# Layer 0's two products as seven block products, one level of Strassen's identity

## The chip, the cores and the metric

The kernel runs on one core of one Trainium2 chip. The metric is the device time of one execution in microseconds; a run of the program gives one such time, and the figure of the kernel is the median of its runs.

## The reference, cut to what matters

Two layers over 1,088 tokens of width 1,024: 1,024 tokens of a prompt and 64 of a running stream. Layer 0 is a gated short convolution, layer 1 an attention over latents, which the change leaves as it is.

```
h = rms_norm(x, norm_g[0])
b_gate, c_gate, xv, z = split(h @ w_in, 4)         # w_in: 1024 x 4096
u = c_gate * xv
conv = up[0:T]*cw[0] + up[1:T+1]*cw[1] + up[2:T+2]*cw[2]   # up: two earlier rows, then u
y = (silu(z) * b_gate * conv) @ w_out              # w_out: 1024 x 1024
x1 = x + y
```

All of it is in float32, and the result has to be as exact as that. TensorE's fast float32 form (fp32r) keeps fewer bits, so the kernel splits each operand into a high part (a cast to fp32r) and a low part (the operand less the high part) and makes every product of three: high by high, high by low, low by high.

## The kernel before, in words

Features lie on the 128 partitions and tokens along the free axis. `XH` and `XL` hold the high and low part of x times the norm's gain, eight tiles of 128 features by 1,088 tokens, resident in SBUF. The tokens are worked on in three chunks of `CHK`: 384, 384 and 320.

Layer 0's input product runs over eight column tiles `ct` and in each over the four parts of w_in in the order 1, 2, 3, 0 (c_gate, xv, z, b_gate). `load_w` brings a weight tile of 128x1024 by DMA (512 KB), ScalarE casts it to the high part (L288) and GpSimd subtracts to give the low part (L292). For each chunk a chain of 24 matmuls (8 feature tiles by 3 products, all through `mm`, L298) sums into one PSUM bank. `conv_evac` (L432 to L467) takes the bank: VectorE multiplies by the norm's factor or by the part before (L440, L451, L457), ScalarE applies silu, two VectorE steps make the convolution (L464), L465 multiplies it by the gate, and the gated result is split into `YH` (ScalarE, L466) and `YL` (GpSimd, L467), which stay in SBUF.

The output product has eight tiles `dt` of one weight tile and three chains of 24 each (`gemm`). Behind each chain VectorE adds the residual from PSUM (L551), and the sum is split into layer 1's `XH` (ScalarE, L552) and `XL` (VectorE, L553, two tensors from SBUF); squares for layer 1's norm are summed at L559.

Nothing is written out by hand here but the start (the first column tile, under `keep_order`): elsewhere the framework's scheduler orders each engine's instructions, and waits follow from data and from buffers (`wraw` has three, `whi` and `wlo` two).

## Time and profile before

| | |
|---|---|
| time, median of 3 runs | 1116.67 us (1116.12 to 1116.78) |
| profiled execution, span | 1115.8 us |
| TensorE (PE), busy | 1075.0 us, 96% |
| VectorE (DVE), busy | 626.8 us, 56% |
| ScalarE (ACT), busy | 502.7 us, 45% |
| GpSimd (POOL), busy | 407.5 us, 37% |
| DMA | 93.18 MB, mean 84 GB/s |

The profiled execution's own time is its span, from its first instruction to its last. PE is the queue of matmuls, PEld that of weight loads beside it. A row that groups instructions names the line, the engine, the operation, the tile written and those read, the shapes, the count, then busy time and the mean of one in ns, and at last the idle time ahead of them with what ended it.

### The profile page before, as it was taken

What the parts mean: (1) busy time and instruction counts of PE and PEld (TensorE: products, weight loads), DVE (VectorE), ACT (ScalarE), POOL (GpSimd) and SP (SyncE); (2) the same over time, 40 slices, a digit from 0 to 9 for tenths busy, and PEclk for the clock granted to TensorE, in tenths of its full rate; (3) what the DMA queues carried; (4) which work ended last, traced back from release to release, by engine and by line L of the source; (5) the groups of instructions that cost most, each with busy time, mean ns of one, the idle gap of its engine ahead of it and who ended that gap; (6) DMA issues with size and microseconds to landing.
All of it is one profiled execution on the core that took longest, in us unless ns stands there. A gap on an engine that the chain in (4) does not pass through costs nothing.

```text
span 1115.8 us, 17727 instructions
## 1 busy us (share of the span) xinstructions
PE 1075.0 (96%) x6659; PEld 1033.5 (93%) x6659; DVE 626.8 (56%) x1277; ACT 502.7 (45%) x1077; POOL 407.5 (37%) x375
## 2 busy tenths in 40 slices
PE   8989999999999999999898999999999999999994
PEld 7989999999999999999798999899999999989983
DVE  6752222222322235554898442688888888896456
ACT  6512121221112133344442334777887778785452
POOL 3123232323324232122433232354555445463243
PEclk9989999999999999999998999999999999999997
DMA  6211111111112123322323113444323422434324
GB/s 228 67 38 39 57 38 43 53 38 50 46 38 77 40 78 139 137 94 90 105 101 124 48 35 86 119 91 103 68 59 91 95 61 51 104 123 151 99 83 153
DMA packets 45461, 93.18 MB, mean 84 GB/s; under 512 B 6672, under 2 KB 23824, under 8 KB 45376
## 3 DMA queue, kind: packets, MB, share of 16 engines
q1 hardware_dynamic: 45168, 91.73, 27.4%
q8 instruction: 52, 0.85, 0.3%
q14 instruction: 33, 0.27, 0.1%
q10 hardware_dynamic: 144, 0.26, 0.1%
q0 software_dynamic: 64, 0.07, 0.0%
HBM read 60.26 MB, written 14.08 MB: 67 GB/s over the span
## 4 chain that ended last, share of the span: by engine, by line
PE 75%; DVE 8%; issue 5%; ACT 4%; DMA 4%; POOL 2%; SPq 1%; POOLq 0%; DVEq 0%; ACTq 0%
PE PS L298 55%; PE PS L1088 16%; PE PS L1127 4%; DMA QB<-stg 2%; POOL wlo L1366 1%; DVE rb L401 1%; ACT PH L1140 1%; DVE PL L1144 1%; SPq L1214 1%; DVE OL L612 1%; DMA wraw<-in_w 1%; ACT stg L1204 1%; DVE qt L813 0%; DVE SZ L364 0%; DVE qt L818 0%
## 5 line engine op out<-in xcount | busy, mean ns | idle before, releaser
L298 PE MATMUL PS<-XH,whi 128*128 128x384 f32 (+1 forms) x984 | 324.2, 329 | 4.7 <-DVE SZ L632 3.9
L298 PE MATMUL PS<-XL,whi 128*128 128x384 f32 (+1 forms) x984 | 322.8, 328 | 0.8 <-DVE XL L392 0.8
L298 PE MATMUL PS<-XH,wlo 128*128 128x384 f32 (+1 forms) x984 | 321.3, 328 | 0.0
L292 POOL TENSOR_TENSOR wlo<-wraw,whi 128x1024 fp32r<-128x1024 f32 x56 | 135.9, 2427 | 301.0 <-ACT whi L288 297.9
L298 PEld LDWEIGHTS PS<-XH,whi 128*128 128x128 f32 x984 | 185.9, 189 | 6.1 <-issue 4.1
L298 PEld LDWEIGHTS PS<-XL,whi 128*128 128x128 f32 x984 | 185.9, 189 | 2.2 <-DVE XL L392 1.8
L298 PEld LDWEIGHTS PS<-XH,wlo 128*128 128x128 f32 x984 | 185.7, 189 | 0.2
L1088 PE MATMUL PS<-KB,QB 96*128 96x512 f32 (+11 forms) x576 | 125.1, 354 | 0.9 <-DVE SZ L632 0.6
L288 ACT CAST whi<-wraw 128x1024 fp32r<-128x1024 f32 (+1 forms) x57 | 59.3, 1040 | 140.4 <-PE PS L298 127.9
L1088 PEld LDWEIGHTS PS<-KB,QB 96*128 96x128 f32 (+1 forms) x576 | 94.4, 190 | 9.3 <-DVE PL L1144 1.1
L1105 DVE TENSOR_REDUCE st<-PS 128x1 f32<-128x1024 f32 (+7 forms) x128 | 94.6, 747 | 10.7 <-PE PS L1088 10.0
L1144 DVE TENSOR_TENSOR PL<-PS,PH 128x512 fp32r<-128x512 f32 (+3 forms) x192 | 98.8, 547 | 3.2 <-ACT PH L1140 1.8
L1122 POOL TENSOR_SCALAR Pt<-Pt,st 128x640 f32<-128x640 f32 (+3 forms) x64 | 61.4, 961 | 85.9 <-DVE st L1118 85.3
L1140 ACT CAST PH<-PS 128x512 fp32r<-128x512 f32 (+3 forms) x192 | 85.3, 496 | 14.6 <-PE PS L1127 13.2
L1088 PE MATMUL PS<-PH,VB 128*128 128x256 f32 x320 | 76.4, 278 | 0.1
L1088 PE MATMUL PS<-PL,VB 128*128 128x256 f32 x320 | 75.2, 281 | 0.2 <-DVE PL L1144 0.2
L1114 ACT ACTIVATE Pt<-PS,st 128x640 f32<-128x640 f32 (+3 forms) x64 | 62.0, 970 | 6.0 <-DVE st L1118 2.9
L298 PE MATMUL PS<-YL,whi 128*128 128x384 f32 (+1 forms) x192 | 63.0, 328 | 0.0
L298 PE MATMUL PS<-YH,whi 128*128 128x384 f32 (+1 forms) x192 | 63.0, 328 | 0.0
L298 PE MATMUL PS<-YH,wlo 128*128 128x384 f32 (+1 forms) x192 | 63.0, 328 | 0.0
L1088 PEld LDWEIGHTS PS<-PH,VB 128*128 128x128 f32 x320 | 60.7, 190 | 1.3 <-DVE PL L1144 0.8
L1088 PEld LDWEIGHTS PS<-PL,VB 128*128 128x128 f32 x320 | 61.0, 191 | 0.7 <-DVE PL L1144 0.4
(339 smaller groups left out, 1963.9 us busy)
## 6 DMA issues: line engine op xcount, KB each, us to landing
wraw<-in_w SPq DMA_DIRECT2D x64, 512.0 KB, 3.4
KB<-stg SPq DMA_DIRECT2D x32, 256.0 KB, 3.9
QB<-stg SPq DMA_DIRECT2D x32, 256.0 KB, 4.3
xr<-in_xT SPq DMA_DIRECT2D x8, 544.0 KB, 4.2
x_scratch<-xr SPq DMA_DIRECT2D x8, 544.0 KB, 2.7
QB<-qr_scratch SPq DMA_DIRECT2D x32, 128.0 KB, 2.9
x<-x_scratch SPq DMA_DIRECT2D x8, 416.0 KB, 3.2
xst<-in_xT SPq DMA_DIRECT2D x16, 192.0 KB, 3.7
```

Source lines behind the costliest of these rows:

```text
L288: ins = A.copy(out=hi[:, :n], in_=raw[:, :n])
L292: ordered((lo_engine or G).tensor_sub(lo[:, :m], raw[:, :m], r32(hi[:, :m])))
L298: ins = PE.matmul(ps, lhsT, rhs, start=start, stop=stop)
L401: ordered(V.tensor_add(rb[:, c0:c1], rb[:, c0:c1], q))
L612: ordered((lo_engine or V).tensor_sub(lo, src, r32(hi)))
L1088: pin(PE.matmul(ps, lhsT, rhs, start=start, stop=stop))
L1105: pin(V.tensor_reduce(out=st[:, 0:1], in_=TL["S", h, i], axis=AX.XY, op=ALU.max, negate=True))
L1114: pin(A.activation(out=Pt, in_=TL.pop(("S", h, i)), func=AF.Exp, bias=st[:, 0:1], accum_out=st[:, 1:2]))
L1122: pin(G.tensor_scalar(Pt, Pt, st[:, 2:3], 1.0, op0=ALU.mult, op1=ALU.mult))
L1127: pin(PE.transpose(out=tp[:, j * P:(j + 1) * P], in_=TL["P", h, i][:, (j0 + j) * P:(j0 + j + 1) * P], identity=ident))
L1140: pin(A.copy(out=hi, in_=src))
L1144: pin(V.tensor_sub(lo, src, r32(hi)))
```

## The change

The tokens are cut into two halves `SC` of 544, each half into two quarters `NS` of 272, the features into two halves of four tiles, and the columns into pairs of weight tiles. On such a two by two block matrix seven products stand in for eight (Strassen's identity in Winograd's form). The first two column tiles of the first token half are still made directly, now in chunks of 272. All else is 36 `Pair`s: 28 of the input product (parts 1 with 2, `put_u`; parts 3 with 0, `put_z`) and 8 of the output product (`out_pair`).

- `build` makes the seven sums of token blocks for each of four feature tiles, with high part (ScalarE) and low part (VectorE); for the input product from x with the norm already applied, for the output product from the DRAM scratch `y_scratch`, where `conv_tail` now writes the gated result.
- `prep` makes the sums of weights for a pair: two loads, three tiles t1, t2, t4 of 512 columns by four VectorE subtractions (L610, L611, L612, L617), and high and low parts of the two whole tiles and of the three sums. The low part of t2 is VectorE's, the four others are GpSimd's (all at L575).
- `product` issues 12 matmuls of 272 columns into one of four banks; p1, p6 and p7 share a bank that goes on summing and are copied to SBUF in between (L638, ScalarE). `put_u` and `put_z` add such a copy to a bank and multiply blocks.
- `run` sets the order: in pair n's turn p1, the last product p3 of pair n-1, p5, p6, p2, p7, p4, with the steps of the next pair's `prep` in between, and `side()` for the builds.
- Layer 1's operands are split behind the output product for the second token half and read back from DRAM for the first (`h_first`).

In layer 0, PE has 2,880 matmuls before (1,920 of 384 columns, 960 of 320), and 3,408 of 272 columns after.

```
+    NS = T // 4
+    SC = 2 * NS
+    REG = 14 * 4 * NS
...
+    y_d = nc.dram_tensor("y_scratch", (KD, P, T), F32, kind="Internal").ap()
...
-    YH = p1.tile([P, KD, T], F32R, name="YH")
-    YL = p1.tile([P, KD, T], F32R, name="YL")
-    rb = p1.tile([P, T], F32, name="rb")
-    rb2 = p1.tile([P, T], F32, name="rb2")
+    R2 = p1.tile([P, REG], F32R, name="R2")
+    SETS = [[R[:, i * REG // 2:(i + 1) * REG // 2].rearrange("p (s k n) -> p s k n", s=7, k=4) for i in range(2)]
+            for R in (R1, R2)]
...
+    def conv_tail(ct, sc, u, z, a, b):
+        n = b - a
+        cv = p1.tile([P, SC], F32, tag="cv", name=nm("cv"), bufs=1)[:, :n]
+        cw = [sm[:, C_CW + j * 8 + ct:C_CW + j * 8 + ct + 1] for j in range(3)]
+        ordered(A.activation(out=cv, in_=u[:, a:b], func=AF.Copy, scale=cw[0]))
+        for j in (1, 2):
+            ordered(V.scalar_tensor_tensor(cv, u[:, a + j:b + j], cw[j], cv, op0=ALU.mult, op1=ALU.add))
...
+        ordered(V.tensor_mul(cv, cv, z[:, a:b]))
+        SP.dma_start(out=y_d[ct][:, sc * SC + a:sc * SC + b], in_=cv)
...
+    def build(sc, k, src, norm):
+        h, l = [x[:, :, k] for x in SETS[sc]]
+        a, b = [STG[:, (2 * (k % 2) + i) * SC:(2 * (k % 2) + i + 1) * SC] for i in range(2)]
+        halves = lambda x: x.rearrange("p (s n) -> p s n", s=2)
+        def put(s, x):
+            o, ol = h[:, s:s + 2], l[:, s:s + 2]
+            A.copy(out=o, in_=halves(x))
+            V.tensor_sub(ol, halves(x), r32(o))
+        SP.dma_start(out=a, in_=src[k][:, sc * SC:(sc + 1) * SC])
+        SP.dma_start(out=b, in_=src[k + 4][:, sc * SC:(sc + 1) * SC])
+        if norm:
+            for x, kk in ((a, k), (b, k + 4)):
+                V.scalar_tensor_tensor(x, x, sm[:, C_NG + kk:C_NG + kk + 1], rb[:, sc * SC:(sc + 1) * SC], op0=ALU.mult, op1=ALU.mult)
+        yield
+        A.copy(out=h[:, 0], in_=a[:, :NS])
+        V.tensor_sub(l[:, 0], a[:, :NS], r32(h[:, 0]))
+        put(1, b)
+        yield
+        V.tensor_add(b[:, NS:], a[:, NS:], b[:, NS:])
+        V.tensor_sub(a[:, NS:], a[:, :NS], a[:, NS:])
+        V.tensor_sub(a[:, :NS], b[:, NS:], a[:, :NS])
+        V.tensor_sub(b[:, :NS], b[:, :NS], a[:, :NS])
+        yield
+        put(3, a)
+        put(5, b)
+        yield
...
+    def parts_of(hi, lo, src, eng):
+        A.copy(out=hi, in_=src)
+        eng.tensor_sub(lo, src, r32(hi))
+        return hi, lo
+    def unit(src):
+        units[0] += 1
+        pool, tags, bufs = (p1, ("bhi", "blo"), 1) if units[0] % 3 == 0 else (wp[0], ("whi", "wlo"), 2)
+        return parts_of(*(pool.tile([P, 1024], F32R, tag=x, name=nm(x), bufs=bufs) for x in tags), src, G)
...
+    def prep(f):
+        ra, rb_ = raw(), raw()
+        SP.dma_start(out=ra, in_=f.srcs[0])
...
+        def own(i):
+            return [p1.tile([P, 512], F32R, tag=f"t{i}{x}", name=nm(f"t{i}{x}"), bufs=1) for x in "hl"]
...
+        def give(u, *names):
+            for j, n in enumerate(names):
+                w[n] = [x[:, j * 512:(j + 1) * 512] for x in u]
+        yield
+        give(unit(ra), "p1", "p2")
+        yield
+        b12, b22 = rb_[:, :512], rb_[:, 512:]
+        b11, b21 = ra[:, :512], ra[:, 512:]
+        t1 = p1.tile([P, 512], F32, tag="t1", name=nm("t1"), bufs=1)
+        V.tensor_sub(t1, b12, b11)
+        V.tensor_sub(b12, b22, b12)
+        V.tensor_sub(b11, b22, t1)
+        give(parts_of(*own(1), t1, G), "p5")
+        yield
+        give(unit(rb_), "p7", "p3")
+        yield
+        V.tensor_sub(b21, b21, b11)
+        give(parts_of(*own(2), b11, V), "p6")
+        give(parts_of(*own(4), b21, G), "p4")
+        yield
...
+    BANK = dict(p1=0, p6=0, p7=0, p2=1, p5=2, p3=2, p4=3)
+    def product(f, name):
+        i = BANK[name]
+        wh, wl = f.w[name]
+        for sc, b in f.banks:
+            ps = PS[:, 4 * b + i, :NS]
+            sh, sl = [x[:, POS[name]] for x in SETS[sc]]
+            for k in range(4):
+                ws = slice(k * P, (k + 1) * P)
+                new = name in ("p1", "p2", "p4", "p5")
+                mm(ps, wh[:, ws], sh[:, k], k == 0 and new, False, not new)
+                mm(ps, wh[:, ws], sl[:, k], False, False, not new)
+                mm(ps, wl[:, ws], sh[:, k], False, k == 3, not new)
+            if i == 0:
+                t = f.tmp[sc, name] = p1.tile([P, NS], F32, tag="k" + name, name=nm(name), bufs=1)
+                A.copy(out=t, in_=ps)
+                if f.early:
+                    f.early(sc, name, t)
+            if name == "p2":
+                f.put(sc, 11, f.tmp[sc, "p1"], ps)
+            elif name == "p7":
+                f.put(sc, 22, t, PS[:, 4 * b + 2, :NS])
+            elif name == "p4":
...
+                f.put(sc, 12, f.tmp[sc, "p6"], ps)
...
+        for n, f in enumerate(pairs):
+            if f.begin:
+                f.begin()
+            while f.whole and jobs:
+                side()
+            product(f, "p1")
+            side()
+            if n:
+                product(pairs[n - 1], "p3")
+                pairs[n - 1].end()
+            step(n + 1)
+            product(f, "p5")
+            side()
+            product(f, "p6")
+            side()
+            step(n + 1)
+            product(f, "p2")
+            side()
+            step(n + 1)
+            product(f, "p7")
+            side()
+            product(f, "p4")
+            side()
+            step(n + 1)
+            step(n + 2)
...
+        def put_u(sc, block, x, ps):
+            q = quarter(block)
+            o = st["u", sc][:, q.start + 2:q.stop + 2]
+            if block % 10 == 1:
+                V.tensor_add(o, x, ps)
+                if ("t", sc, q.start) in st:
+                    V.tensor_mul(o, o, st.pop(("t", sc, q.start)))
+                else:
+                    st["d", sc, q.start] = True
+            else:
+                t = p1.tile([P, NS], F32, tag="t", name=nm("t"), bufs=2)
+                V.tensor_add(t, x, ps)
+                if ("d", sc, q.start) in st:
+                    V.tensor_mul(o, o, t)
+                else:
+                    st["t", sc, q.start] = t
...
+        def end_u():
+            for sc in scs:
+                conv_state(ct, sc, st["u", sc])
+        def end_z():
+            for sc in scs:
+                conv_tail(ct, sc, st["u", sc], st["z", sc], 0, SC)
+            if ct == KD - 1:
+                jobs.extend(build(scs[0], k, y_d, False) for k in range(4))
...
-    for ct in range(KD):
...
+    for ct in range(2):
...
+    jobs.append(second_half())
+    single = lambda cts, sc: [f for ct in cts for f in conv_pairs(ct, [sc])]
+    pairs = single(range(2, KD), 0) + single(range(KD), 1)
...
+    def h_first():
+        for dt in range(KD):
+            x = p1.tile([P, SC], F32, tag="cv", name=nm("hx"), bufs=1)
+            SP.dma_start(out=x, in_=x1_d[dt][:, :SC])
+            h_split(dt, 0, SC, x)
+            yield
...
+        def early(sc, name, t):
+            if name == "p1":
+                G.tensor_add(xr[0][:, :NS], xr[0][:, :NS], t)
+        def put(sc, block, t, ps):
+            a, j = block // 10 - 1, block % 10 - 1
+            dt = 2 * q + j
+            x = xr[j][:, a * NS:(a + 1) * NS]
+            if block != 11:
+                V.tensor_add(x, x, t)
+            V.tensor_add(x, ps, x)
+            c0 = sc * SC + a * NS
+            SP.dma_start(out=x1_d[dt][:, c0:c0 + NS], in_=x)
+            if sc == 1:
+                h_split(dt, c0, c0 + NS, x)
+            if c0 not in begun:
+                begun.add(c0)
+                A.activation(out=acc1[:, c0:c0 + NS], in_=x, func=AF.Square)
+            else:
+                s = p1.tile([P, NS], F32, tag="t", name=nm("sq"), bufs=2)
+                A.activation(out=s, in_=x, func=AF.Square)
+                V.tensor_add(acc1[:, c0:c0 + NS], acc1[:, c0:c0 + NS], s)
...
+    pairs += [out_pair(q, sc) for sc in range(2) for q in range(4)]
+    for i in (12, len(pairs) - 8, len(pairs) - 4):
+        pairs[i].whole = True
+    run(pairs)
...
-    for dt in range(KD):
-        wh, wl = load_w(w2[dt], 1024)
-        xr = p1.tile([P, T + 4], F32, tag="u", name=nm("xr"), bufs=2)
-        SP.dma_start(out=xr[:, :T], in_=xT[dt])
...
-        for c, (c0, c1) in enumerate(CHK):
-            n = c1 - c0
-            ps = gps()
-            gemm(ps[:, :n],
-                 lambda k: wh[:, k * P:(k + 1) * P], lambda k: wl[:, k * P:(k + 1) * P],
-                 lambda k: YH[:, k, c0:c1], lambda k: YL[:, k, c0:c1], KD)
-            V.tensor_add(xr[:, c0:c1], ps[:, :n], xr[:, c0:c1])
-            at = A.activation(out=XH[:, dt, c0:c1], in_=xr[:, c0:c1], func=AF.Copy, scale=g)
-            V.scalar_tensor_tensor(XL[:, dt, c0:c1], xr[:, c0:c1], g, r32(XH[:, dt, c0:c1]), op0=ALU.mult, op1=ALU.subtract)
```

GpSimd's order, before, around one weight tile of the input product (`wlo` is a weight tile's low part, `YL` the gated result's, one row for each chunk):

```order
L292 TENSOR_TENSOR wlo_168_2531<-wraw_166_2529,whi_167_2530 128x1024
L453 TENSOR_TENSOR z_158_2417<-z_158_2417,rb_105 128x320
L467 TENSOR_TENSOR YL_104<-cv_162_2451,YH_103 128x384
L467 TENSOR_TENSOR YL_104<-cv_163_2483,YH_103 128x384
L292 TENSOR_TENSOR wlo_171_2613<-wraw_169_2611,whi_170_2612 128x1024
```

And in the change, for one pair and the start of the next (`t1l` and `t4l` are low parts of weight sums, `blo` is a third buffer for a weight tile's low part):

```order
L575 TENSOR_TENSOR wlo_235_2086<-braw_222_1993,whi_234_2085 128x1024
L575 TENSOR_TENSOR t4l_241_2125<-wraw_221_1992,t4h_240_2124 128x512
L575 TENSOR_TENSOR blo_247_2163<-wraw_242_2128,bhi_246_2162 128x1024
L575 TENSOR_TENSOR t1l_251_2197<-t1_249_2192,t1h_250_2196 128x512
L575 TENSOR_TENSOR wlo_253_2215<-wraw_243_2129,whi_252_2214 128x1024
L575 TENSOR_TENSOR t4l_259_2255<-wraw_242_2128,t4h_258_2254 128x512
```

The gated result's low part is gone from GpSimd; a pair has two whole low parts and two of half a tile.

VectorE's order in the change, at the turn of a pair of parts 1 and 2 (`wraw` and `braw` are the raw weight tiles in which the sums are made in place; p1, p6 and p7 are the copies from PSUM):

```order
L739 TENSOR_TENSOR t_226_2025<-p6_209_1924,PS_64 128x272
L741 TENSOR_TENSOR z_185_1732<-z_185_1732,t_226_2025 128x272
L472 TENSOR_TENSOR cv_227_2028<-cv_227_2028,z_185_1732 128x544
L612 TENSOR_TENSOR wraw_221_1992<-braw_222_1993,t1_231_2064 128x512
L617 TENSOR_TENSOR wraw_221_1992<-wraw_221_1992 128x512
L610 TENSOR_TENSOR t1_249_2192<-wraw_243_2129,wraw_242_2128 128x512
L575 TENSOR_TENSOR t2l_239_2121<-wraw_221_1992,t2h_238_2120 128x512
L611 TENSOR_TENSOR wraw_243_2129<-wraw_243_2129 128x512
L714 TENSOR_TENSOR u_223_1996<-p1_225_2011,PS_64 128x272
L721 TENSOR_TENSOR t_237_2103<-p7_236_2101,PS_64 128x272
```

Five operations of 512 columns that take two inputs from SBUF have come into VectorE's turn, between those that empty the banks.

ScalarE's order in the change, at the same place (`bhi`, `whi`, `t1h`, `t2h`, `t4h` are high parts):

```order
L638 COPY p1_225_2011<-PS_64 128x272
L574 CAST whi_228_2034<-wraw_221_1992 128x1024
L574 CAST t1h_232_2068<-t1_231_2064 128x512
L574 CAST t2h_238_2120<-wraw_221_1992 128x512
L638 COPY p6_230_2062<-PS_64 128x272
L574 CAST whi_234_2085<-braw_222_1993 128x1024
L638 COPY p7_236_2101<-PS_64 128x272
L574 CAST t4h_240_2124<-wraw_221_1992 128x512
```

The cast of t2 stands right ahead of the copy of p6; t2 is written by L612 into the raw tile that GpSimd's `wlo` of the same tile reads.

## Rows read from the trace of the kernel before

**Rows 1.** The page's head.

```profile
span 1115.8 us, 17727 instructions
```

**Rows 2.** The chain that ended last, in order of time: start, length, engine, line, count.

```profile
64.81 434.73 PE PS L298 x2622
```

**Rows 3.** Windows of layer 0: the first line names the columns.

```profile
core 0: us, PE busy (x) PEld busy (x) DVE busy (x) ACT busy (x) POOL busy (x), PEclk, DMA share, GB/s
6.00:20.00 14.00, 12.38 (x65) 10.88 (x64) 9.67 (x13) 9.35 (x19) 6.97 (x5) 1.00 0.80 284
60.00:65.00 5.00, 0.62 (x4) 0.35 (x4) 4.44 (x10) 1.14 (x2) 3.29 (x2) 0.84 0.23 71
65.00:70.00 5.00, 5.00 (x21) 5.00 (x22) 2.11 (x8) 1.30 (x4) 0.33 (x1) 0.50 0.23 85
...
100.00:400.00 300.00, 300.00 (x1822) 300.00 (x1821) 75.72 (x179) 58.33 (x91) 98.33 (x65) 1.00 0.15 48
```

**Rows 4.** PE's timeline, first matmuls of chains: start, us, line, shape.

```profile
146.88 0.33 PE L298 MATMUL PS<-XH,whi 128*128 128x384 f32 x1
...
151.04 0.31 PE L298 MATMUL PS<-XH,whi 128*128 128x320 f32 x1
...
154.56 0.34 PE L298 MATMUL PS<-XH,whi 128*128 128x384 f32 x1
...
719.55 0.28 PE L1088 MATMUL PS<-PH,VB 128*128 128x256 f32 x1
...
720.97 0.22 PE L1088 MATMUL PS<-PH,VB 128*128 128x128 f32 x1
```

**Rows 5.** Groups by line and shape in layer 0, from 0 to 520 us.

```profile
L292 POOL TENSOR_TENSOR wlo<-wraw,whi 128x1024 fp32r<-128x1024 f32 x39 | 93.5, 2398 | 238.4 <-ACT whi L288 238.4
L284 POOL TENSOR_TENSOR wlo<-wraw,whi 128x512 fp32r<-128x512 f32 x2 | 2.6, 1298 | 3.6 <-ACT whi L283 3.6
L288 ACT CAST whi<-wraw 128x1024 fp32r<-128x1024 f32 x39 | 41.0, 1051 | 123.2 <-PE PS L298 112.2 <-issue 11.1
L283 ACT CAST whi<-wraw 128x512 fp32r<-128x512 f32 x2 | 1.1, 617 | 0.7 <-DMA wraw<-in_w 0.7
L343 ACT COPY rb<-PS 128x384 f32<-128x384 f32 x2 | 0.9, 458 | 0.0
L465 DVE TENSOR_TENSOR cv<-cv,z 128x384 f32<-128x384 f32 x16 | 8.9, 558 | 0.6
L553 DVE SCALAR_TENSOR_TENSOR XL<-xr,sm,XH 128x320 fp32r<-128x320 f32 x8 | 18.7, 2344 | 6.9 <-ACT XH L552 6.9
L392 DVE SCALAR_TENSOR_TENSOR XL<-xst,sm,XH 128x320 fp32r<-128x320 f32 x8 | 4.3, 547 | 1.5 <-ACT XH L391 1.5
```

**Rows 6.** Timelines of VectorE and GpSimd at three places where both have work.

```profile
488.63 2.41 POOL L292 TENSOR_TENSOR wlo<-wraw,whi 128x1024 fp32r<-128x1024 f32 x1 [9.57 <-ACT whi L288]
489.04 2.34 DVE L553 SCALAR_TENSOR_TENSOR XL<-xr,sm,XH 128x320 fp32r<-128x320 f32 x1 [0.95 <-ACT XH L552]
...
1080.10 5.10 POOL L1366 TENSOR_TENSOR wlo<-wraw,whi 128x1024 fp32r<-128x1024 f32 x2 [2.58 <-ACT whi L1364]
1087.84 2.70 POOL L1366 TENSOR_TENSOR wlo<-wraw,whi 128x1024 fp32r<-128x1024 f32 x1
1082.96 8.94 DVE L1338 TENSOR_TENSOR X<-X,acc 128x384 f32<-128x384 f32 x5
...
1097.95 3.22 DVE L1338 TENSOR_TENSOR X<-X,acc 128x448 f32<-128x448 f32 x6
1097.95 5.42 POOL L1366 TENSOR_TENSOR wlo<-wraw,whi 128x1024 fp32r<-128x1024 f32 x1 [7.41 <-ACT whi L1364]
```

**Rows 7.** The same two engines, VectorE with one input from PSUM.

```profile
843.63 0.59 POOL L1122 TENSOR_SCALAR Ph<-Ph,st 128x384 f32<-128x384 f32 x1 [0.25 <-DVE st L1118]
843.79 0.69 DVE L1208 TENSOR_TENSOR stg<-PS,stg 128x512 fp32r<-128x512 f32 x1 [0.26 <-ACT stg L1204]
```

**Rows 8.** PE's waits from 0 to 70 us: releaser, total, count, longest.

```profile
PE PS L298 <- DVE rsy L330: 5.9, 2, 4.4
```

More of the change, by code (lines that the diff above doesn't have):

```diff
@@ new lines, with side, load_half @@
+    jobs = []
+    def side(n=1):
+        while n and jobs:
+            if next(jobs[0], 0) == 0:
+                jobs.pop(0)
+            else:
+                n -= 1
+    def load_half():
+        for k in range(KD):
+            x = STG[:, (k % 4) * SC:(k % 4 + 1) * SC]
+            SP.dma_start(out=x, in_=xT[k][:, SC:])
+            if k == 0:
+                A.activation(out=rb[:, SC:], in_=x, func=AF.Square)
+            else:
+                A.activation(out=x, in_=x, func=AF.Square)
+                V.tensor_add(rb[:, SC:], rb[:, SC:], x)
+            if k % 2:
+                yield
@@ new lines, in run, with step @@
+    def run(pairs):
+        bset = 0
+        steps = {}
+        for n, f in enumerate(pairs):
+            if len(f.scs) == 1:
+                f.banks = [(f.scs[0], bset)]
+                bset = 1 - bset
+            else:
+                f.banks = [(f.scs[0], 0), (f.scs[1], 1)]
+        def step(n, k=1):
+            for _ in range(k):
+                if n < len(pairs):
+                    if n not in steps:
+                        steps[n] = prep(pairs[n])
+                    next(steps[n], None)
+        step(0, 5)
+        step(1, 1)
+        for n, f in enumerate(pairs):
+            if f.begin:
[22 more added lines that the diff above has]
+            step(n + 2)
+        product(pairs[-1], "p3")
+        pairs[-1].end()
+        while jobs:
+            side()
@@ L475 @@
+    PARTS = [1, 2, 3, 0]
+    for ct in range(2):
+        u, z = new_u(ct, 0), new_z()
         if ct == 0:
@@ L497 @@
             pe_order[0] = True
-            held = {c: [] for c in range(3)}
+            held = {c: [] for c in range(2)}
             held[0].append(conv_mm(0, W[1], 3))
@@ L502 @@
                     x_square(0, k)
-                W[part] = load_w(w1[ct][part], 1024, into=(YH[:, 6 + part // 3, :1024], YL[:, 6 + part // 3, :1024]))
-            for c in range(3):
+                W[part] = load_w(w1[ct][part], 1024, into=[p1.tile([P, 1024], F32R, tag=x, name=nm(x), bufs=1) for x in ("bhi", "blo")] if part else
+                                 [R1[:, REG - n:REG - n + 1024] for n in (2048, 1024)])
+            for c in range(2):
                 for pi, part in enumerate(PARTS):
@@ L517 @@
                         for q in range(3):
-                            conv_evac(ct, u, zt, PARTS[q], c, held[c][q])
+                            conv_evac(ct, u, z, PARTS[q], c, held[c][q])
                     if pi == 3:
-                        conv_evac(ct, u, zt, part, c, held[c][3])
-            pe_order[0] = False
+                        conv_evac(ct, u, z, part, c, held[c][3])
             keep_order[0] = False
+            jobs.extend(build(0, k, xT, True) for k in range(4))
         else:
@@ L525, with second_half @@
                 W = load_w(w1[ct][part], 1024)
-                for c in range(3):
-                    conv_evac(ct, u, zt, part, c, conv_mm(c, W))
-    SP.dma_start(out=o_conv, in_=nconv.rearrange("p a b -> p (a b)"))
-    acc1 = const.tile([P, T], F32, name="acc1")
+                for c in range(2):
+                    conv_evac(ct, u, z, part, c, conv_mm(c, W))
+                    side(2)
+        conv_state(ct, 0, u)
+    while jobs:
+        side()
+    split_psum(g=(7, 8))
+    def second_half():
+        yield from load_half()
+        yield
+        yield
+        end = rstd([rb[:, SC:]], rb[:, SC:], D, SC)
+        yield
+        yield
+        yield
+        end()
+        yield
+        for k in range(4):
+            yield from build(1, k, xT, True)
+    jobs.append(second_half())
+    single = lambda cts, sc: [f for ct in cts for f in conv_pairs(ct, [sc])]
+    pairs = single(range(2, KD), 0) + single(range(KD), 1)
     parts = {}
@@ L662 @@
     held = latent_mm(0, 0)
-    sums(2, p3t.tile([P, 512], F32, tag="qt1", name=nm("act"), bufs=2))
+    for c in (1, 2):
+        sums(c, p3t.tile([P, 512], F32, tag="qt1", name=nm("act"), bufs=2))
     latent_evac(0, 0, held)
```

241 lines of the change are left out of this document (156 added, 85 removed).

## The prediction

> **What bounds the kernel now.** I read the page's head first, then the chain that ended last, then windows of layer 0, then single timelines for prices. The profiled execution's span is 1115.8 us [rows 1], 0.9 us under the median of 1116.67; the sum below is a difference, made against this execution, and is added to the median. The chain shows TensorE alone from 64.81 us for 434.73 us, so layer 0 ends at 499.5 us [rows 2]. In the window from 100 to 400 us PE is busy for all 300 us at granted clock 1.00 (2.4 GHz), while VectorE is busy for 75.72 and GpSimd for 98.33 [rows 3]. Layer 0 is therefore PE's, and VectorE and GpSimd together need 174 of 300 us. The reader should keep that sum in mind, since it is the one that the change moves.
>
> **What the change takes from PE.** From the first matmul of one chain of 24 to that of the next, PE needs 151.04 - 146.88 = 4.16 us at 384 columns, 173.3 ns each, and 154.56 - 151.04 = 3.52 us at 320, 146.7 ns each; twelve matmuls of 256 columns take 720.97 - 719.55 = 1.42 us, 118.3 ns each [rows 4]. Between 320 and 256 columns, 272 come to 118.3 + 16/64 x 28.4 = 125.4 ns. Layer 0's matmuls before: 1,920 x 173.3 + 960 x 146.7 = 473.5 us. After: 3,408 x 125.4 = 427.4 us. The difference is 46 us in favour of the change, not an eighth, because smaller matmuls cost more for each column and the first two column tiles of a half stay direct. A pair takes PE 84 x 125.4 = 10.5 us; the same work, two weight tiles on half of the tokens, takes 48 x 173.3 + 24 x 146.7 = 11.84 us before.
>
> **What it adds to GpSimd.** Each weight tile is now used for 544 tokens at a time and so is split twice. A pair has two low parts of 1,024 columns at 2,398 ns and two of 512 at 1,298 ns [rows 5]: 7.4 us, for 36 pairs 266 us. The direct column tiles add 8 x 2.4 = 19 us, and eight early adds and four multiplications of 272 columns some 0.7 us each (1,298 x 272 / 512) = 8 us. Together 293 us. By itself that would hide under 427 us of PE.
>
> **What it adds to VectorE.** I count only operations whose two inputs both lie in SBUF, in columns: prep 36 x 5 x 512 = 92,000; the 16 builds 16 x 11 x 272 = 48,000 for low parts and sums, and 9,000 for the norm; multiplications of blocks 56 x 272 = 15,000; the tails of the convolution 14 x 3 x 544 = 23,000; the output product's adds, squares and splits 23,000; the second half's squares 4,000; the start and the direct tiles 11,000. Together 225,000. The 384-column one took 558 ns by itself, 1.45 ns for each column [rows 5]: 327 us. Additions that read a bank come on top, some 70 us, and by themselves these too would hide.
>
> **Why the two don't hide.** At 489.04 us a 320-column L553 starts 0.41 us after a GpSimd low part of 2.41 us; it takes 2.34 us and ends 0.34 us after that. The mean of its eight is 2,344 ns, where the same operation in the start (L392) takes 547 [rows 5, 6]. From 1082.96 us five VectorE operations of 384 columns take 8.94 us beside GpSimd's stream, one getting through for each GpSimd operation, whose pitch is then 2.70 us. And at 1097.95 us six VectorE operations of 448 columns run in 3.22 us, while the low part that began with them takes 5.42 us, 3.02 more than the usual 2.40 [rows 5, 6]. So one engine works while the other stands. With one input from PSUM it isn't so: at 843.79 us such an operation took 0.69 us across the end of a GpSimd one [rows 7]. The additions that read a bank are free of it. Before the change this costs nothing: 174 us of 300 leave room. After it the shared path is a queue of its own.
>
> **Its price.** Three rows bound what a VectorE column costs on that path. In a row behind each other: 3.02 us / (6 x 448) = 1.12 ns, 253 us. As whole operations: 1.45 ns, 327 us. Taking turns with GpSimd: (2.70 - 2.40) us / 384 = 0.78 ns, 176 us [rows 5, 6]. There are some 590 such operations to 167 of GpSimd, so most stand behind another of their own; I take 1.12.
>
> The Trainium skill ("SBUF — State Buffer", section "Who interferes with whom") says that a VectorE instruction with two SBUF inputs contends with a GpSimd instruction that reads SBUF, and that whoever issues first holds the shared pair for the whole instruction. The trace agrees on who blocks whom; by "the whole instruction" the sum would go by 327 us, where the six operations in a row cost 1.12 ns and not 1.45, and the measurement decides.
>
> **The sum.** Shared path: 253 + 293 = 546 us. To this come about 6 us at the start, before the window in which the loads run at 284 GB/s [rows 3], and time in which neither can run because both wait for a ScalarE cast. In GpSimd's order for a pair every low part waits for its cast, and t1, t2 and t4 wait for VectorE ahead of it. Casts take 1,051 ns for a tile and 617 for half a one [rows 5]. The trace of before doesn't show how much stands bare: at least nothing, at most all five, 2 x 1.05 + 3 x 0.62 = 4 us for each pair, 143 us. I take one half-tile cast, 0.62 x 36 = 22 us, because the next pair's tiles are asked for a turn ahead. Layer 0 then ends at 546 + 6 + 22 = 574 us, 74.5 us after before's 499.5, and all that follows moves with it: **1116.7 + 74.5, about 1191 us.** PE, with 454 us of its own (499.5 - 46), waits some 120 us of this: behind a VectorE operation that is held stand the additions that empty the banks (L714, L721, L739 in VectorE's order), and PE's next product into that bank waits for them, as its products with t1, t2 and t4 wait for late low parts.
>
> Edits that cost nothing: the gated result's way through DRAM, since pairs lie between its writing and its reading and GpSimd gave up that low part; the loads, 1 MB for each pair in about 14 us, some 75 GB/s where 284 were moved in the window from 6 to 20 us [rows 3]; ScalarE, whose casts and copies of a pair come to about 2 x 1.05 + 3 x 0.62 + 3 x 0.4 = 5 us of work. If that cover goes, the shared path still is the longer.
>
> **Rivals.**
> *A, the other side: PE sets the pace.* The shared path decides only while a pair's share of it is over PE's 10.5 us. The conv pair's own is 7.4 us of GpSimd and about 3,630 columns, 4.1 us at 1.12: 11.5 us, near that point. The builds and the output product carry the rest. If the low parts and the sums overlapped more than rows 6 show, PE would decide: 1116.7 - 46 = 1071 without waits. ScalarE's order adds a wait: the cast of t2 stands ahead of the copy of p6 in 16 of the 36 turns, and before it come a 1.05 us cast, a 2.40 us low part, a VectorE subtraction of 512 x 1.45 = 0.74, the cast itself and the copy, 0.62 + 0.45 [rows 5], 5.26 us in all. If the chain begins behind p1 and p3 (24 x 0.125 = 3.0 us), it ends at 8.3 us of the turn, where p7 is due after 60 matmuls, at 7.5. That is 0.8 x 16 = 13 us. The first build in front of pair 0, some 4 x 4.6 us of VectorE, may cost another 8. So 1071 to 1092. Against it stands every row of 6. **Chance 0.11.**
> *B, the two engines mesh well.* Half of the columns go at the alternating price, 88 + 126 = 214 us, and no cast stands bare: 214 + 293 = 507, 7.5 us over before, 1124 us. The long run of turns at 1082.96 us speaks for it; that VectorE has three or four of its own in a row speaks against. **Chance 0.12.**
> *C, the clock falls too.* Behind a PE wait of 4.4 us [rows 8] the granted clock was 0.84 and in the next 5 us 0.50 (1.2 GHz) [rows 3], so half of 5 us was lost. In my forecast PE waits 120 / 36 = 3.3 us for each pair. If these waits come in one piece, the fall costs 2.5 us of PE in each turn, and since the copies, adds and buffers wait for PE in turn, half to all of it may come on top: 45 to 90 us, 1236 to 1281. Against it: in the window from 6 to 20 us, with 1.6 us of waits, the clock stayed at 1.00 [rows 3]. **Chance 0.12.**
> *D, whole operations and more bare casts.* With 1.45 ns for each column: 327 + 293 + 28 = 648, 148.5 over, 1265 us. **Chance 0.08.**
> *No change*, A's gain and the new waits cancelling: **0.04.** That the change wouldn't do what it says is ruled out by the count of matmuls.
>
> **How the numbers follow.** The forecast, 0.53, is 1191 us; its own bounds are B's 1124 and D's 1265. The range runs from 1124 to 1275: it leaves out A (0.11), no change (0.04) and the upper end of C (about 0.04). Over 0.2% (2.2 us, about what a measurement of this kernel can tell): faster 0.11, from A; same 0.04; slower 0.85, from the forecast, B, C and D.
>
> **What would show it.** Right: layer 0 ends near 574 us; PE is busy for some 75% of it, with waits for VectorE and ScalarE in every pair; the low parts of weights last well over 2.4 us, their mean 3 us or more; L610 to L617 show times of 2 us or more where GpSimd's run; L714 and L721, which read a bank, keep under 0.6 us when they start. Wrong: a mean low part of 2.4 us and PE busy over 95% of layer 0 would be A; granted clocks of 0.5 to 0.8 in layer 0 would be C. A layer 1 that lasts other than before's 616 us (1115.8 - 499.5) by more than 5 us would show a part that I did not cost.

## The result, and the profile after

The changed kernel takes 1272.2 us, median of 4 runs (1270.05 to 1273.87), against 1116.7 in the same session: a ratio of 1.139 [1.1375, 1.1407], the brackets holding its 95% interval, as for the runs below. It is slower by 155 us, just inside the range of 1124 to 1275 and on the side that was forecast, but more than twice as far as the forecast of 1191.

The head, the busy times, the granted clock in 40 slices and the shares of the chain, from the page of after; before's span is [rows 1]:

```profile
span 1269.8 us, 20253 instructions
...
PE 1092.9 (86%) x7195; PEld 1041.3 (82%) x7195; DVE 1014.8 (80%) x1702; ACT 657.8 (52%) x1376; POOL 599.5 (47%) x451
...
PEclk8978889898988898998999989999999999999997
...
PE 45%; DVE 36%; issue 8%; ACT 4%; POOL 3%; DMA 3%; SPq 1%; POOLq 0%; DVEq 0%; ACTq 0%
```

The last product of layer 0 ends near 655 us, before's at 499.5 [rows 2], and what follows takes 614.8 us against 616.3, so all of the loss lies in layer 0. Windows of after; the columns are those of [rows 3]:

```profile
0.00:65.00 65.00, 56.14 (x382) 54.50 (x383) 48.13 (x109) 32.15 (x62) 22.56 (x19) 0.92 0.50 159
65.00:655.00 590.00, 452.21 (x3102) 440.46 (x3101) 528.00 (x707) 257.80 (x466) 317.21 (x157) 0.89 0.33 107
```

From 65 us on VectorE is busy for 528 of 590 us and PE for 452, where before's row from 100 to 400 us has 75.72 and 300 of 300 [rows 3]. PE has given up the pace. VectorE's 528 us are not all work. Timelines of GpSimd and VectorE in one turn of a pair of after (start, length):

```profile
375.36 2.40 POOL L575 TENSOR_TENSOR blo<-wraw,bhi 128x1024 fp32r<-128x1024 f32 x1 [5.04 <-ACT bhi L574]
377.71 1.76 POOL L575 TENSOR_TENSOR t1l<-t,t1h 128x512 fp32r<-128x512 f32 x1
382.04 2.75 POOL L575 TENSOR_TENSOR wlo<-braw,whi 128x1024 fp32r<-128x1024 f32 x1 [2.57 <-ACT whi L574]
```

```profile
375.41 2.93 DVE L472 TENSOR_TENSOR cv<-cv,z 128x544 f32<-128x544 f32 x1
378.26 1.76 DVE L612 TENSOR_TENSOR wraw<-braw,t 128x512 f32<-128x512 f32 x1
380.06 0.69 DVE L617 TENSOR_TENSOR wraw<-wraw 128x512 f32<-128x512 f32 x1
...
382.47 0.43 DVE L714 TENSOR_TENSOR u<-p,PS 128x272 f32<-128x272 f32 x1
382.82 2.00 DVE L479 COPY u<-carry 128x2 f32<-128x2 f32 x1
384.74 0.42 DVE L721 TENSOR_TENSOR t<-p,PS 128x272 f32<-128x272 f32 x1
```

L472 starts with the low part `blo` and ends 0.58 us after it, one operation of 544 columns late. The next low part, `t1l`, stands while L472 works and so takes 1.76 us and not 1.30 [rows 5]; L612 waits for `t1l`, and L617, with GpSimd idle, takes 0.69. L714, which reads a bank, takes 0.43 beside a low part. This is the taking of turns of [rows 6]. PE stands behind it (waits up to 655 us):

```profile
PE PS L299 <- DVE t L739: 40.4, 11, 3.9
PE PS L299 <- ACT p L638: 40.3, 21, 5.2
PE PS L299 <- DVE z L886: 17.1, 7, 5.4
PE PS L299 <- DVE t L721: 13.5, 4, 4.6
```

So the mechanism is there; the sum is not. From the starts and ends in the trace, each instant counted once, layer 0's 655 us divide into three (below, this is called the count):

| us of layer 0 | forecast | after |
|---|---|---|
| GpSimd or a two-input operation of VectorE at work | 546 | 564.6 |
| only another operation of VectorE (bank additions, above all) | 0 | 41.5 |
| neither engine at work | 28 | 48.9 |
| layer 0 | 574 | 655 |

By the same count PE is busy for 46.8 of the 48.9 us in the third row and ScalarE for 17.4: that time is mostly a product that is waited for.

### The profile page after: what moved, and what is told of

It reads as the page before. It is cut to its first block, busy times and chain, and to the rows that moved or that the text cites. A ratio compares the mean times of both kernels' runs of the same rounds, so it can differ in the third digit from the quotient of the medians.

```text
span 1269.8 us, 20253 instructions
## 1 busy us (share of the span) xinstructions
PE 1092.9 (86%) x7195; PEld 1041.3 (82%) x7195; DVE 1014.8 (80%) x1702; ACT 657.8 (52%) x1376; POOL 599.5 (47%) x451
## 4 chain that ended last, share of the span: by engine, by line
PE 45%; DVE 36%; issue 8%; ACT 4%; POOL 3%; DMA 3%; SPq 1%; POOLq 0%; DVEq 0%; ACTq 0%
PE PS L299 27%; PE PS L1442 14%; PE PS L1481 4%; DVE wraw L612 3%; DVE cv L464 3%; DVE R L519 2%; DVE cv L472 2%; DVE cv L471 2%; DMA QB<-stg 2%; DVE acc L897 2%; DVE t L610 1%; DVE wraw L617 1%; POOL wlo L1720 1%; DVE t2l L575 1%; DVE braw L611 1%
## 5 line engine op out<-in xcount | busy, mean ns | idle before, releaser
L299 PE MATMUL PS<-R,whi 128*128 128x272 f32 (+2 forms) x1422 | 329.1, 320 | 82.5 <-DVE t L739 29.2
L299 PEld LDWEIGHTS PS<-R,whi 128*128 128x128 f32 x1422 | 249.1, 203 | 90.9 <-DVE t L739 30.9
L299 PE MATMUL PS<-R,wlo 128*128 128x272 f32 (+1 forms) x744 | 235.2, 318 | 1.5 <-POOL wlo L575 1.3
L299 PEld LDWEIGHTS PS<-R,wlo 128*128 128x128 f32 x744 | 150.5, 203 | 2.1 <-POOL wlo L575 1.6
L575 POOL TENSOR_TENSOR wlo<-wraw,whi 128x1024 fp32r<-128x1024 f32 x36 | 90.9, 2525 | 95.5 <-ACT whi L574 84.4
L299 PE MATMUL PS<-R,bhi 128*128 128x272 f32 x416 | 89.2, 312 | 36.6 <-ACT p L638 12.7
L299 PEld LDWEIGHTS PS<-R,bhi 128*128 128x128 f32 x416 | 71.1, 206 | 40.0 <-ACT p L638 14.3
L575 POOL TENSOR_TENSOR t1l<-t,t1h 128x512 fp32r<-128x512 f32 x36 | 62.3, 1730 | 27.3 <-ACT t1h L574 20.7
L575 POOL TENSOR_TENSOR t4l<-wraw,t4h 128x512 fp32r<-128x512 f32 x36 | 55.2, 1532 | 40.1 <-ACT t4h L574 40.0
L299 PE MATMUL PS<-R,t1h 128*128 128x272 f32 x288 | 65.1, 322 | 9.7 <-ACT R L518 8.7
L575 POOL TENSOR_TENSOR blo<-wraw,bhi 128x1024 fp32r<-128x1024 f32 x18 | 45.1, 2506 | 45.6 <-ACT bhi L574 39.7
L299 PE MATMUL PS<-R,blo 128*128 128x272 f32 x208 | 63.4, 310 | 0.0
```

Source lines behind the costliest of these rows:

```text
L299: ins = PE.matmul(ps, lhsT, rhs, start=start, stop=stop, skip_group_check=more)
L575: eng.tensor_sub(lo, src, r32(hi))
```

## The experiments

The theory: operations of VectorE that read two inputs from SBUF and GpSimd's take turns, and their sum sets layer 0. The rivals: VectorE simply has too much work of its own; the order on ScalarE makes PE wait; the granted clock falls.

**lo_vector: the low parts on VectorE.**

```
-        ... for x in tags), src, G)
+        ... for x in tags), src, V)
-        give(parts_of(*own(1), t1, G), "p5")     # and the same for own(4)
+        give(parts_of(*own(1), t1, V), "p5")
```

> The low parts of the pairs' weights (two of 1,024 columns and two of 512 for each of 36 pairs) move from GpSimd to VectorE; nothing else changes. Shared path: VectorE and GpSimd take turns whenever VectorE reads two tensors from SBUF, so the time of GpSimd's low parts (266 us at 2.40 and 1.30 us) leaves the path and 110,600 columns at 1.12 ns, 124 us, join it: about 140 us less, 1130 us, within 1105 to 1160. VectorE's own work: VectorE is busy 92% of layer 0 because it has that much to do, and what it is given adds to it: 124 us more, about 1395 us. Order: what counts is how long a pair's chain of casts and low parts is; the low parts become shorter but queue behind VectorE's other work, so between 1230 and 1300 us.

1151.05 us, ratio 1.030 [1.0281, 1.0322]: VectorE was given 144 more operations, and the kernel became 121 us faster. That VectorE had too much of its own is out, and so is the order as the main cause (1230 to 1300). Three of its groups by line and shape in layer 0 (count, busy us, mean ns), then its window from 65 us to layer 0's end:

```profile
L575 DVE TENSOR_TENSOR wlo<-wraw,whi 128x1024 fp32r<-128x1024 f32 x36 | 44.3, 1230 | 0.4
...
L617 DVE TENSOR_TENSOR wraw<-wraw 128x512 f32<-128x512 f32 x36 | 24.6, 684 | 0.0
...
L464 DVE SCALAR_TENSOR_TENSOR cv<-u,sm,cv 128x544 f32<-128x544 f32 x28 | 21.8, 778 | 0.0
```

```profile
65.00:534.00 469.00, 420.19 (x3110) 415.17 (x3109) 450.76 (x850) 262.50 (x466) 19.97 (x13) 0.93 0.43 135
```

The last two of these groups in after:

```profile
L464 DVE SCALAR_TENSOR_TENSOR cv<-u,sm,cv 128x544 f32<-128x544 f32 x28 | 41.5, 1482 | 8.2 <-ACT cv L462 8.2
L617 DVE TENSOR_TENSOR wraw<-wraw 128x512 f32<-128x512 f32 x36 | 33.5, 931 | 0.5
```

A low part of 1,024 columns takes VectorE 1,230 ns where GpSimd takes 2,398 [rows 5], and operations that nobody touched are shorter by 247 and 704 ns. VectorE is busy for 451 of 469 us now, nearly all of it work.

**lo_zero: GpSimd writes and doesn't read.**

```
-        eng.tensor_sub(lo, src, r32(hi))
+        if eng is G:
+            G.memset(r32(lo), 0.0)
+        else:
+            eng.tensor_sub(lo, src, r32(hi))
```

> GpSimd writes zeros where the low parts of the pairs' weights stood (two whole tiles and t1 and t4), reading nothing: that part of the products is left out; t2's low part and all that VectorE, ScalarE and PE do stays. Shared path: nothing is left for VectorE to wait for; its own queue, 253 us at 1.12 ns for each column and 95 us of bank additions and small ones, falls under PE's 454, and PE sets the pace: 1075 to 1110 us. VectorE's own work: VectorE's operations keep their durations, about 1272 us. Order: the casts and copies still wait for each other, but no low part is waited for: 1150 to 1220 us.

1102.53 us, 0.987 [0.9847, 0.9891]. GpSimd still works, with writes. One group of GpSimd and one of VectorE in layer 0, then the window from 65 us:

```profile
L576 POOL MEMSET wlo<- 128x1024 f32 x48 | 45.8, 955 | 111.2 <-PE PS L299 111.1
```

```profile
L620 DVE TENSOR_TENSOR wraw<-wraw 128x512 f32<-128x512 f32 x36 | 24.7, 687 | 0.4
```

```profile
65.00:484.00 419.00, 400.70 (x3100) 396.54 (x3099) 335.96 (x705) 257.79 (x465) 121.14 (x154) 0.98 0.47 150
```

L620 (after's L617) takes 687 ns with GpSimd busy for 121 of 419 us, as it takes 684 in lo_vector, where GpSimd is mostly idle. It isn't that the two seldom meet: 14 of the 36 run beside a memset for 0.3 us or more, and take 680 to 694 ns. One of them:

```profile
134.10 0.96 POOL L576 MEMSET wlo<- 128x1024 f32 x1 [2.44 <-PE PS L299]
```

```profile
134.59 0.68 DVE L620 TENSOR_TENSOR wraw<-wraw 128x512 f32<-128x512 f32 x1
```

The Trainium skill ("SBUF — State Buffer", section "Who interferes with whom") says that the contention is with a GpSimd instruction that reads SBUF and not with one that only writes it; this run agrees. PE is busy for 401 of 419 us: this is PE's pace, and rival A's price for it (1071 to 1092) was 10 us too low at its upper end.

**no_sums: three of four subtractions left out**, by deleting L611, L612 and L617.

> Three of the four VectorE subtractions that make the sums of weights (L611, L612, L617) are left out, so t2 and t4 hold weights that are not sums; 108 operations and 55,300 columns fewer. Shared path: 55,300 columns at 1.12 ns leave the path, 62 us, to 1210 us (1195 to 1225). VectorE's own work: their busy time leaves with them, 50.7 + 32 + 33.5 = 116 us, to 1156 us. Order: the cast of t2 waited 73 us for L612 and needs to no more: 1200 us, and PE's waits for ScalarE's copies (40 us) go.

1196.09 us, 1.071 [1.067, 1.0744]: 76 us less for 55,300 columns, 1.38 ns for each, between the shared path's 62 and the 116 of the durations. It doesn't tell the shared path from the order (1200).

**act_kept: ScalarE in program order**, by `tc.keep_in_program_order` around the casts (L574) and the copies (L638).

> ScalarE's casts of weights and copies of banks keep the order of the program, so the copy of p6 no longer stands behind the cast of t2; no work changes. Shared path: the path is as long as before, 1272 us within 15. Order: PE's waits for ScalarE's copies, 40 us in layer 0, go: about 1235 us.

1259.05 us, 1.127 [1.1254, 1.1287]: 13 us less, a third of what the order was to give and within what the path left open. In after, the cast of t2, which stands ahead of p6's copy, itself waited for VectorE's L612; in act_kept PE waits less for the copies and more for VectorE's L721 (13.5 us in after). A group of ScalarE in after, then two of PE's waits in act_kept's layer 0:

```profile
L574 ACT CAST t2h<-wraw 128x512 fp32r<-128x512 f32 x36 | 22.3, 619 | 74.8 <-DVE wraw L612 73.4 <-DVE u L501 1.4
```

```profile
PE PS L299 <- DVE t L721: 40.9, 13, 3.8
PE PS L299 <- ACT p L638: 24.7, 12, 3.3
```

**no_bank and no_small: VectorE's other operations.** In no_bank ScalarE copies the bank (`A.copy(out=t, in_=ps)` for `V.tensor_add(t, x, ps)` in `put_u` and `put_z`). In no_small the operations of two columns that carry and mend the convolution's state are deleted.

> The 112 additions of the input product that read a bank and a copy (L714, L721, L731, L739, 430 ns each, 48 us) are left out: ScalarE copies the bank instead, so the copies of p1, p6 and p7 are not added in. Bank additions not hidden: in the profile of after VectorE and GpSimd together are at work for 606 us of layer 0's 655, and 565 of it is two-input work or GpSimd's, so 41 of 95 us of VectorE's other operations stand alone: 20 to 48 us less, 1225 to 1252. Hidden, as the prediction had it: 1264 to 1280, or more by ScalarE's 42 us.

> Operations of two columns that carry the convolution's state over the halves and mend the seam are left out (L468 to L471, L477 to L481; the state output is zeros): 72 on VectorE, busy for 54 us in the profile of after, up to 2 us each where GpSimd runs. Held time counts once, with GpSimd's work: 0 to 20 us less, 1252 to 1272. Held time counts in VectorE's queue, since what stands behind waits: about 54 us less, 1218.

no_bank: 1256.33 us, 1.125 [1.123, 1.1275], 16 less: more than if these additions were hidden (up to 8), less than the 20 to 48. By the count above, the time of VectorE's other operations alone falls from 41.5 to 15.2 us, and that in which neither engine works rises from 48.9 to 60.1: part of the place is taken by waits for ScalarE's copies (PE's come to 87 us, 40 in after). no_small: 1261.79 us, 1.130 [1.1279, 1.1324], 10 less of the 53 for which these operations, 56 and not 72, were busy: held time counts once, with GpSimd's work.

**out_direct and direct_first: parts undone.** In out_direct the gated result is read back from DRAM, split (`y_split`) and multiplied by `gemm` in chunks of 272; in direct_first the loop over direct column tiles runs to `KD`, and only the second half has pairs.

> The output product is made directly again, on the two token halves in chunks of 272 from the gated result in DRAM, split when it is read back: a part of the change undone. Shared path: 42,000 VectorE columns at 1.21 ns (51 us) and 27 us of GpSimd leave, with some 11 us of the time in which neither works; PE gets 12 us more: about 1183 us (1165 to 1200). If the loss were in the input product alone: 1272 + 12 = 1284.

> The first token half's input product is made directly for all eight column tiles, and only the second half's (16 pairs) and the output product's (8) are block products: a part of the change undone. Shared path: VectorE's columns with two SBUF inputs fall from 225,000 to about 171,000, at 1.21 ns (what the profile of after gives: 564.6 us of path less 293) 207 us; GpSimd has 24 x 7.4 + 32 x 2.4 + 17 = 272 us; bank additions that stand alone 40 and time in which neither works 35: layer 0 554 us, in all about 1171 us (1145 to 1190). VectorE's own work: its busy time would fall by 54,000 columns of two inputs, about 65 us, to 1205. PE's share rises to 445 us in either case.

out_direct: 1227.09 us, 1.099 [1.0969, 1.1013]; 45 less where 89 were expected. direct_first: 1230.36, 1.102 [1.0994, 1.1042]; 42 less where 101 were. Both parts lose time in after, but the sum over the whole layer is a bad guide here, as two windows of direct_first show:

```profile
20.00:220.00 200.00, 184.62 (x1428) 183.10 (x1429) 110.00 (x220) 64.24 (x103) 81.61 (x42) 0.97 0.35 119
220.00:616.00 396.00, 307.63 (x2110) 299.82 (x2110) 352.83 (x470) 174.69 (x321) 218.71 (x109) 0.90 0.33 109
```

In the direct stretch PE is busy for 185 of 200 us and VectorE's spare 90 us go unused; in the stretch of pairs it is 89% busy. Time saved on the path counts only in the stretches that the path sets.

**filler, filler2 and no_wl_mm: the clock, and PE's part.** The fillers are matmuls that nobody reads, behind each product:

```
+            for _ in range(3):
+                mm(PS[:, 4 * (1 - b) + 1, NS:512], onesr, SETS[f.banks[0][0]][0][:, 0, 0, :512 - NS], True, True, True)
```

In filler they were four and went to the product's own bank (`4 * b + i`). no_wl_mm drops `mm(ps, wl[:, ws], sh[:, k], ...)` from `product`.

> Behind each of the seven products of a pair, PE makes four matmuls of 240 columns into a part of the bank that nobody reads: 28 for each pair, about 0.11 us each at the upper clock, 3.2 us of PE in turns that last 15 us with 10.6 us of work; what is computed stays the same. Shared path: PE's spare time takes them; the time stays within 15 us of 1272, more if anything. Clock: the granted clock in layer 0 (0.85 to 0.93 in most windows) rises towards 1.00 and the products that the path waits for get faster; if the falls were what the sum lacked (81 us), 1200 to 1250 us.

> As filler, but the matmuls nobody reads (three of 240 columns behind each product, 21 for each pair, about 2.4 us of PE at the upper clock) go to the other pair's bank of p2, which was read a turn ago, so they wait for no copy; what the pairs compute stays. Clock: granted clocks in layer 0 rise and the products on the path get faster; if the falls made the part that the forecast lacked (81 us), 1200 to 1245. Sum of the shared path, bank additions and bare time: PE has 4 us to spare for each pair, so within 10 us of 1272, or up to 40 us more where the fillers stand in front of a product that the path waits for.

> The third product of each block, low part of the weights by high part of the tokens, is left out on PE alone (28 of a pair's 84 matmuls, 126 us of PE at the upper clock); GpSimd and VectorE still make all the low parts. PE off the path: within 10 us of 1272. PE on the path with the share that the chain of waits gives it (23% of layer 0, 152 us): a third of that, 50 us less, about 1222. Clock the cause: PE waits more, the clock falls further, no gain or a loss.

filler: 1451.09 us, 1.300 [1.2967, 1.3022], and inconclusive: the fillers stood behind the copy out of their own bank (PE's waits for ScalarE's copies are 110 us in the first 560 us, against 40 in all of after's layer 0), and unlike the expectation has it they changed what is computed. filler2: 1302.41 us, 1.167 [1.1643, 1.1686]. no_wl_mm: 1228.34 us, 1.100 [1.0981, 1.1021]. From 65 us to the end of layer 0, filler2 and then no_wl_mm:

```profile
65.00:685.00 620.00, 513.92 (x3858) 502.51 (x3857) 494.30 (x707) 259.27 (x466) 313.79 (x157) 0.94 0.32 102
```

```profile
65.00:611.00 546.00, 346.69 (x2123) 333.07 (x2122) 526.25 (x706) 255.32 (x466) 318.56 (x157) 0.82 0.35 116
```

With the clock at 0.94, up from 0.89, the time rose by 30 us, within the 40 that the path allowed for fillers in front of a product; with the clock at 0.82 it fell by 44. The mean clock by itself doesn't set the time; since both runs also change PE's work, they don't say what the falls cost. What no_wl_mm does show is that PE's matmuls were on the path: with a third of the pairs' gone VectorE is busy for 526 of 546 us. (It also spares PE the wait for low parts, but in after that is 6 us, 1.3 for GpSimd's and 4.5 for `t2l`.) By the count, the shared path is 560.3 us (564.6 in after), VectorE's other operations alone 30.3 (41.5), neither 20.4 (48.9). Nearly all of the 44 us come out of the last two: time in which the adds and copies waited for a product.

**Towards a better version.** direct_first_lov is direct_first with lo_vector's edit. dual_lov is lo_vector with both token halves in one turn for column tiles 4 to 7, so that their weights are prepared once, and two buffers for each kind of copy:

```
-    pairs = single(range(2, KD), 0) + single(range(KD), 1)
+    pairs = single(range(2, 4), 0) + [f for ct in range(4, KD) for f in conv_pairs(ct, [0, 1])] + single(range(4), 1)
```

dual_lov_od is dual_lov with out_direct's output product. mix makes column tiles 2 and 3 of the first half directly too; od_kept is dual_lov_od with act_kept's order; od_three is between mix and dual_lov_od (column tile 2 alone), with act_kept's order too.

> The same with the pairs' low parts on VectorE. Shared path: VectorE 171,000 + 74,000 columns at 1.21 ns = 296 us, bank additions and small ones 95, GpSimd's low parts of the direct tiles 94: 470 to 505 us for layer 0, about 1105 us (1087 to 1122). VectorE's own work: 74,000 columns more than the version without, 90 us later than that one.

> Low parts on VectorE as in lo_vector, and the input product of column tiles 4 to 7 takes both token halves in one turn, so that 28 sets of weight sums and parts are made and not 36 (8 x 5,632 columns of VectorE fewer); PE's matmuls are the same. Shared path, where VectorE is now the queue that decides (99% busy in layer 0 with lo_vector): 45,000 columns at 1.21 ns, 54 us off 1151: about 1097 us (1085 to 1115). Order: eight banks taken in one turn leave none free for the next, and the copies wait: 1130 to 1170.

> dual_lov with the output product direct as in out_direct: block products only where they use a prepared pair well. Shared path, VectorE's queue: of the 142 us that the output product takes in dual_lov, VectorE full, 67,000 columns leave, and PE's 768 matmuls at 125.4 ns, 96 us, set the pace: 46 us off 1142.6, about 1096 us (1085 to 1112), under the kernel before. Order: the direct product waits for the gated result's way through DRAM at the seams, 1115 to 1135.

> dual_lov_od with the first token half of column tiles 2 and 3 made directly too, so that the second half's norm is made beside direct products, where VectorE has room, and its sums stand bare ahead of the first pair (about 20 us). In dual_lov_od the window from 65 to 150 us, four single pairs and these sums, takes 85 us for 55 us of PE's matmuls with VectorE full; direct products take 48 us, with 20 for the sums 68: 17 us off 1120, about 1103 us (1095 to 1115), under the kernel before. If the clock falls behind the bare sums, up to 5 us more.

> dual_lov_od with ScalarE's casts and copies kept in the order of the program, as in act_kept, where that gave 13 us. Order: the copies that PE waits for in the single pairs come earlier: 5 to 10 us less, 1110 to 1115. Path: VectorE is full in the stretch from 65 to 150 us whatever ScalarE does, and elsewhere PE waits for nothing: 1120 within 4.

> The first token half direct for column tiles 0 to 2, two single pairs for tile 3 in front of the double ones, ScalarE in program order. The second half's norm is made beside the direct products; its sums (20 us of VectorE) fall into two single pairs (21 us of PE, some 42 of VectorE). Path: VectorE's need up to the first double pair is what counts, as in dual_lov_od and mix, so between them, 1118 to 1126. If direct tiles hid their VectorE work wholly: 1105 to 1112.

direct_first_lov 1148.72 us, 1.029 [1.0268, 1.0314]; dual_lov 1142.6, 1.023 [1.0205, 1.0261]; dual_lov_od 1120.31, 1.0038 [1.0024, 1.0052]; mix 1127.49, 1.010 [1.0087, 1.0119]; od_kept 1127.58, 1.009 [1.0075, 1.0113]; od_three 1126.82, 1.009 [1.0074, 1.0103]. Against the upper ends of the path's ranges all came out slow, od_three by under a microsecond and the others by 4 to 28, and none is faster than the kernel before. Two lie in the range that was given for the order (dual_lov and dual_lov_od), but not for its reason: PE doesn't wait for banks in dual_lov's double pairs, nor at the seams of dual_lov_od, which lie behind 150 us. dual_lov in the stretch of its double pairs:

```profile
150.00:330.00 180.00, 179.22 (x1421) 179.00 (x1421) 131.87 (x260) 72.09 (x134) 0.00 (x0) 1.00 0.21 74
```

Windows of dual_lov_od, the best:

```profile
20.00:65.00 45.00, 39.95 (x283) 39.52 (x284) 36.51 (x85) 19.83 (x38) 13.63 (x7) 0.89 0.38 124
65.00:150.00 85.00, 65.45 (x437) 63.29 (x436) 80.88 (x158) 44.47 (x79) 3.78 (x3) 0.87 0.41 132
150.00:500.00 350.00, 349.80 (x2767) 349.43 (x2767) 264.10 (x479) 158.75 (x284) 40.81 (x17) 1.00 0.37 123
```

From 150 us on PE is full at clock 1.00, so there fewer matmuls can shorten the time. Ahead of it the sums of token blocks and four single pairs fill VectorE, 81 of 85 us, and PE makes 437 recorded matmuls, 55 us at 125.4 ns, in 85. In mix PE idles later, and not behind VectorE alone: from 100 to 200 us it is busy for 84 us and VectorE for 64. Why od_kept, where act_kept's order had given 13 us, is 7 us slower than dual_lov_od, stays open.

## Why the prediction was wrong

- *What bounds the kernel before, and PE's share:* right. In lo_zero, with the path out of the way, PE was busy for 455 of layer 0's 484 us, where the prediction had 454 of its own; with its waits that is 14 us under before, not 46.
- *That VectorE and GpSimd take turns:* right, by lo_vector and lo_zero.
- *Its price:* 1.12 ns for a column was a little low. In after (564.6 - 293) / 225,000 = 1.21 ns; in lo_vector a low part costs 1,230 / 1,024 = 1.20. That is 19 of the 81 us that were missing. The price by whole operations, 1.45, was too high, so that rival D came near the time (1265) for a reason that isn't so. That the range, which reaches up to D, holds the time is luck.
- **The step that failed is the sum**, in two terms. The first: "The additions that read a bank are free of it." They aren't held (432 ns on the mean, below), but they stand in VectorE's queue, and GpSimd didn't always have work just then: of 95 us of VectorE's operations other than two-input ones, 41.5 stood alone and were priced at nothing. no_bank took away 26 of these, though the time fell by 16 only.
- The second is time in which neither works, "one half-tile cast, 0.62 x 36 = 22 us", with 6 for the start: 48.9 measured. I looked for it in ScalarE's casts, and took PE to be covered, with 120 us to spare. But it is PE that is busy in 46.8 us of it: adds wait for a product, and the next low part and product wait behind the adds. no_wl_mm brought this term to 20.4 us without touching a cast (from 39 to 9 from 65 us on), and the other operations that stood alone to 30.3.
- *Rival C:* its 1236 to 1281 holds the time, and the clock did fall (0.89 from 65 us on): of PE's 508 busy us, 119 ran at 0.50. But 88 of these lay beside work of the shared path, and only 22 in the time in which neither other engine works; at 1.00 those would be 11 us shorter, an estimate, against C's 45 to 90. What the falls cost by delaying the additions that stood alone (9 of the 119 us) or by changing the order of the queues stays open, and so does how much of no_wl_mm's 44 us belongs to the clock.
- *Rival A:* its order on ScalarE was priced at 13 us, and act_kept gave 13. The rival's figure was for a turn that PE sets, so the agreement may be chance. A conv pair's own columns are also 2,560 + 544 + 816 = 3,920 and not 3,630, which puts its share of the path at 11.8 us and not 11.5.
- *What would show it:* PE's share (508 us of 655, 78%) and L714's and L721's times (432 ns) came as said, and layer 1 kept its length. Two signs did not come: the whole low parts lasted 2.59 us on the mean and not 3, and L610 to L617 reached 2 us in 9 of 144 cases, with means from 0.72 to 1.41 by shape. GpSimd was held less than was said, by its half low parts most (`t1l` 1,730 ns where 1,298 were read). Groups of after in layer 0:

```profile
L575 POOL TENSOR_TENSOR wlo<-wraw,whi 128x1024 fp32r<-128x1024 f32 x36 | 90.9, 2525 | 95.5 <-ACT whi L574 84.4
L575 POOL TENSOR_TENSOR t1l<-t,t1h 128x512 fp32r<-128x512 f32 x36 | 62.3, 1730 | 27.3 <-ACT t1h L574 20.7
```

```profile
L612 DVE TENSOR_TENSOR wraw<-wraw,t 128x512 f32<-128x512 f32 x18 | 25.4, 1412 | 0.0
...
L714 DVE TENSOR_TENSOR u<-p,PS 128x272 f32<-128x272 f32 x28 | 12.1, 432 | 5.9 <-PE PS L299 5.9
```

## What to carry to other kernels

Price added VectorE work together with GpSimd's as one queue wherever VectorE reads two tensors from SBUF while GpSimd reads SBUF too, and look whether the work is shorter on VectorE alone: here 1.23 us against 2.40 made the same kernel 121 us faster. Sum such a path stretch by stretch, since what one stretch saves another can't use. And where the engines are closely matched, don't take the longest alone: add what stands in its queue beside the shared work, and the round trip through the engine that seems to be covered.
